# Four pairs of a projection by half products, and a planner that prices two engines by intervals

## The chip, the cores and the metric

The kernel runs on one core of a Trainium2 chip. The metric is the device time of one execution in microseconds. Three runs of the kernel before gave 671.8, 672.92 and 673.86 us; their median, 672.92 us, stands for it. Smaller is better. All data are float32. A matrix product is made as three products of high and low parts (`hi*hi`, `hi*lo`, `lo*hi`) in the format that TensorE reads at full pace, so every weight and every activation is first split in two by ScalarE (a copy that rounds) and VectorE (a subtraction).

## The reference

One decoder layer: 512 tokens of width 1024, a pooling mixer and an attention with 8 heads of 64, each merged by its own gate, then a feed-forward part of width 2816. What the change touches is `y_nsa`, the attention's output times `w_nsa_out` (512 rows, 1024 columns):

```python
y_nsa = nsa_mixer(...) @ w_nsa_out[l]                       # (512, 512) @ (512, 1024)
x = x + (gate_pool * y_pool + gate_nsa * y_nsa) @ w_out[l]
h = rms_norm(x, ffn_norm_g[l])
gate_pre, val = jnp.split(h @ w_up[l], 2, axis=-1)
x = x + (jax.nn.silu(causal_dwconv(gate_pre, conv_w[l], conv_b[l])) * val) @ w_down[l]
```

## The kernel before

The stages follow each other: input projection; attention, head by head, with the feature stream beside it (key and value features, pooling, gates and `y_pool`); `y_nsa`; the product with `w_out`; 22 blocks of `up`, among them parts of `down`; the rest of `down`. Activations lie transposed, features on 128 partitions and 512 tokens along a row, so an output feature block is 128x512 in one PSUM bank.

**Who sets the order.** The kernel is not written in the order in which it runs. Every operation is noted by a class `Plan` (line 120 on) with its engine, its tiles and a price, and at the end `emit` (391) runs a list schedule over all of them several times, keeps the order that ends first over a few assumed speeds of transfers, and issues each engine's instructions in it. All instructions therefore carry one line in the profile, L434. `price` (206) returns three numbers: how long the operation occupies its engine (`cost`), how much later its result is there (`tail`), and the bytes of a transfer. In `run` the engine is free again at start plus `cost` (343); a consumer on another engine may start at start plus `cost` plus `tail` plus 0.06 us, and one on the same engine at start plus `cost` (266). `dues` (376) then gives each operation of VectorE, ScalarE and the queues a time by which TensorE needs it, and the next round picks by those times. TensorE has two streams in fixed order of their own: `m` (attention and all behind it) and `f` (the feature stream); the planner only chooses which of the two goes next, keeping their progress about equal. A bank of PSUM or a page of SBUF is given out again when its last reader has run; the weights pass through three rings of three buffers (`wraw`, `whi`, `wlo`).

**Attention.** For each head `scores` (1058) makes scores on TensorE, their minimum on VectorE, exponentials on ScalarE, and normalizes on VectorE; `transposes` turns the blocks on TensorE and splits them into `pt` and `pz`; `av` (1098) multiplies with the values into the single bank `av`, its last product being `av<-ptc`; `av_out` (1125) empties that bank: ScalarE copies one half to `ot`, VectorE adds it to the other, giving `oraw`. Products of the feature stream stand between these steps. The gates are `th`; the products `mm<-xh,whi` and `mm<-yph,whi` belong to that stream.

**`y_nsa`.** Its 1024 output features are four pairs `c` of two blocks of 128. A pair that is in `FASTM` (line 58: 0 and 1) is done by half products, a scheme that makes seven products of half height where the plain way makes eight: the pair's weights are cut into four pieces and, by sums of pieces on VectorE (`s3`, `wraw`), recombined into seven; the attention's output is recombined likewise, once (`half_sums`, 1113, giving `osh` and `osl`). Each half product is two steps of three matmuls of 128x256 (`product`, 1177), so a pair has 42. Between them ScalarE and VectorE copy and add halves (`u`, `mm<-tr`). The last two products of a pair (`end1`, `end2`) are held and issued among the next pair's products. Pairs 2 and 3 go the plain way: two blocks of four steps of three matmuls of 128x512, 24 in all. Either way a block is then gated (`tn`, read back from DRAM with `gp`) and split into `mh` and `ml`, the operand of the product with `w_out`.

**`w_out` and on.** For features 0 and 4 the product starts over the first six columns of `mh`, `ml`, before the last two are there (line 1319); then all eight features are finished, residual added (`x`), and split for `up`. Block 0 of `up` is plain, the others go by half products.

Of the kernel before, what the change touches and what calls it, by code (L numbers as in the profile page):

```python
# [19 lines left out]
KD = 8  # L20
# [34 lines left out]
RINGS = {"wraw": 3, "whi": 3, "wlo": 3}  # L55
PLAIN = (0,)
DIRECT = (0,)
FASTM = (0, 1)
AT = (6, 11, 16)
FILL = {f: (0, 0, 0, 0) for f in range(22)}  # L60
FILL.update({f: (0, 1, 1, 0) for f in (7, 9, 10)})
# [30 lines left out]
def _cols(x):  # L92
    n = 1
    for _, c in list(x.ap)[1:]:
        n *= c
    return n
# [23 lines left out]
class Plan:  # L120
# [3 lines left out]
    def __init__(self, nc):  # L124
        self.real = {"PE": nc.tensor, "ACT": nc.scalar, "DVE": nc.vector, "POOL": nc.gpsimd, "SP": nc.sync}
        self.engines = [Engine(self, n) for n in ("PE", "ACT", "DVE", "POOL", "SP")]
        self.ops, self.tag, self.writes, self.reads, self.users = [], {}, {}, {}, {}
        self.caps, self.rank, self.count, self.psum, self.early = {}, {}, {}, set(), {}
        self.fine = set()
        self.stream, self.open, self.after = "m", None, []  # L130
        self.span, self.lead, self.base = [0, 0], LEAD, BASE

# [73 lines left out]
    def price(self, eng, method, outs, ins, a, kw):  # L206
        n = max(_cols(x) for x in outs + ins)
        if method == "dma_start":
            x = outs[0]
            size = x.ap[0][1] * _cols(x) * 4 if hasattr(x, "ap") else 0  # L210
            return (0.87 if eng == "POOL" else 0.45), 0.0, size * (2.0 if kw.get("accum_op") is not None else 1.0)
        if eng == "PE":
            n = _cols(a[2])
            return max(n / 2250.0 + (0.005 if n < 300 else 0.0), 0.109), 0.17, 0
        if eng == "ACT":
            c = 0.19 + n * 0.000835
            if any(_cols(x) == 1 for x in ins):
                c += 0.09
            if kw.get("accum_out") is not None:
                c += 0.19  # L220
            if a[2] in (AF.Sin,):
                c += 1.28
            return c, 0.0, 0
        if eng == "DVE":
            wide = [x for x in ins if _cols(x) > 1]
            if method == "tensor_tensor_reduce":
                return 0.24 + n * 0.00105, 0.0, 0
            if len(wide) > 1 or method == "tensor_reduce" or any(x.tensor.name in self.psum for x in wide):
                return 0.15 + n * (0.00105 if method != "scalar_tensor_tensor" else 0.00114), 0.0, 0
            return 0.2 + n * 0.00054, 0.0, 0  # L230
        if method == "memset":
            return 0.1 + n * 0.0008, 0.0, 0
        return 0.33 + n * 0.0025, 0.0, 0
# [204 lines left out]
def hybrid_layer(ctx: ExitStack, tc: tile.TileContext, xT, xa, pos, par, cst, poolw, w1, wa, wb, wf,  # L438
                 wpo, wno, wout, wup, wdn, wdh, wdz, out):
    nc = tc.nc  # L440
    pl = Plan(nc)
# [49 lines left out]
    def mm3(pt, wh, wl, xh, xl, k0, k1, koff=0, nk=None, first=0):  # L491
        nk = k1 if nk is None else nk
        for k in range(k0, k1):
            c = slice((k - koff) * P, (k - koff + 1) * P)
            with pl.unit():
                PE.matmul(pt, wh[:, c], xh[k], start=(k == first), stop=False)
                PE.matmul(pt, wh[:, c], xl[k], start=False, stop=False)
                PE.matmul(pt, wl[:, c], xh[k], start=False, stop=(k == nk - 1))
# [208 lines left out]
    for t in range(NT):  # L707
        pt = bank("mm")
        tk = slice(t * P, (t + 1) * P)
        for k in range(KD):  # L710
            wh, wl = bw[k]
# [200 lines left out]
    for i in range(2):  # L912
# [8 lines left out]
        for q in range(4):  # L921
            hi, lo = page("w1h", dt=F32R), page("w1l", dt=F32R)
            split(hi, lo, w1t[q])
            for l in range(2 * q, 2 * q + 2):
                c = slice((l % 2) * 256, (l % 2 + 1) * 256)
# [83 lines left out]
    def cmp_scores(g):  # L1009
        cps[g] = page("cs", (P, 4, P))  # L1010
        tmp = page("ct", (P, 4, P))
        for j in range(2):
            pt = bank("tr")
            pq = pt.rearrange("p (q a t) -> p q a t", q=2, a=2)
            with pl.unit():
                for i in range(2):
                    for a in range(2):
                        PE.matmul(pq[:, :, a], kz[:, g, i], QT[a, 2 * j + i][:, 2 * g:2 * g + 2], start=(i + a == 0),
                                  stop=(i == 1), skip_group_check=True)
            r, o = slice(j * 64, (j + 1) * 64), slice((1 - j) * 64, (2 - j) * 64)  # L1020
            t, c = (x.rearrange("p a b -> p (a b)") for x in (tmp, cps[g]))
            ACT.activation(t[r], pt[o], AF.Copy)
            DVE.tensor_add(c[r], pt[r], t[r])
# [34 lines left out]
    def scores(h, i):  # L1058
        g, hh = divmod(h, 4)
        n = i + 1  # L1060
        pt = bank("sc", (P, 4, 2, P)) if n > 2 else bank("tr", (P, 2, 2, P))
        with pl.unit():
            for j in range(0, n, 2):
                m = min(2, n - j)
                for s in range(2):
                    PE.matmul(pt[:, j:j + m], QT[h % 2, i][:, h // 2], KT[s, j // 2, g][:, 0:m], start=(s == 0), stop=(s == 1),
                              skip_group_check=True)
        x = pl.tile(sb, (P, 8, 2, 64), F32, "pp", "ppb", 4) if n > 2 else pl.tile(sb, (P, 4, 2, 64), F32, "pp", "ppa", 2)
        sm = keep("asm", (P, 4, 2), bufs=4)
        pp = [x[:, :2 * n, b].rearrange("p (j u) k -> p j u k", u=2) for b in range(2)]  # L1070
        pt = pt[:, 0:n].rearrange("p j b (u k) -> p j b u k", u=2)
        rows = mask[:, NT - n:NT].rearrange("p j (u k) -> p j u k", u=2)
        for b in range(2):
            DVE.tensor_tensor_reduce(out=pp[b], in0=pt[:, :, b], in1=rows, scale=1.0,
                                     scalar=3.0e38, op0=ALU.add, op1=ALU.min, accum_out=sm[:, 0, b:b + 1])
        for b in range(2):
            ACT.activation(pp[b], pp[b], AF.Exp, bias=sm[:, 0, b:b + 1], scale=-1.0,
                           accum_out=sm[:, 1, b:b + 1])
        DVE.reciprocal(sm[:, 2], sm[:, 1])
        DVE.tensor_mul(sm[:, 3], sm[:, 2], gates[:, i, 3 * h + 1:3 * h + 3])  # L1080
        for b in range(2):
            DVE.tensor_scalar_mul(pp[b], pp[b], sm[:, 3, b:b + 1])
        Pt[h, i] = x
# [54 lines left out]

    compress_kt()
    scores(0, 0)  # L1140
    cmp_scores(0)
    cmp_scores(1)
    scores(0, 1)
# [43 lines left out]
    mh, ml, nots, held = [None] * KD, [None] * KD, [], []  # L1187
# [9 lines left out]
    for c in range(4):  # L1197
        if c not in FASTM:
            more = list(held)
            del held[:]  # L1200
            wh, wl = weights(flat(wno[c]), 1024, "v")
# [80 lines left out]

        held.extend((end1, end2))
        tail = nots[-1]
    for q in held:
        q()

    x2, gh, gl, begun = [None] * KD, [None] * KD, [None] * KD, []
    acc = page("acc")
# [29 lines left out]
    for f in (0, 4):  # L1319
        wh, wl = weights(flat(wout[f]), 1024, "v")  # L1320
        begin[f] = wh, wl, any_bank()
        mm3(begin[f][2], wh, wl, mh, ml, 0, 6, nk=KD)
    for f in (0, 4, 1, 5, 2, 6, 3, 7):
        xres = page("xres")
        with pl.behind(tail):
# [254 lines left out]
        held.extend((end1, end2))  # L1580

    for f in range(KF):
        if f in AT:
            g = AT.index(f)
            (hp_group if g == HALVED else dn_group)(g)
        fill(FILL[f][0], True)
        if f in PLAIN:
            up_plain(f)
        else:
            up_fast(f, *FILL[f][1:])  # L1590
# [140 lines left out]
```

## Time and profile before

| what | before |
|---|---|
| median of three runs, us | 672.92 (671.8 to 673.86) |
| the profiled execution, us | 672.4 |
| its span from first to last instruction, us | 670.6 |
| granted TensorE clock | 1.000 |
| TensorE busy, us (share) | 665.8 (99%) |
| VectorE busy, us | 568.5 (85%) |
| ScalarE busy, us | 470.5 (70%) |
| GpSimd busy, us | 111.8 (17%) |
| VectorE busy from head 0's `oraw` to head 4's (139.25 to 215.94) | 63.34 of 76.69 |
| VectorE busy from the last `oraw` to the first `x` (262.31 to 297.77) | 30.14 of 35.46 |

In a row of the timeline stand the start in us from the span's start, the duration, the engine (PE is TensorE, PEld its weight loads, DVE VectorE, ACT ScalarE, POOL GpSimd, SP the engine whose queue most transfers use), the operation, the written tile and those read, the shapes, how many, and in brackets how long the engine had been idle and what ended that. Names of tiles on TensorE carry the PSUM tag of the bank (`mm`, `tr`, `av`, `sc`). Instructions of one engine may overlap, so a duration is not the distance to the next start. TensorE's products are pipelined: their durations overlap, their starts give the pitch.

### The profile page before, as it was taken

How to read it: one execution, taken by the hardware profiler on the slowest of the kernel's cores; microseconds unless marked ns; L12 is line 12 of the kernel's file. 1: busy time of each engine (PE TensorE's matmuls, PEld its weight loads, DVE VectorE, ACT ScalarE, POOL GpSimd, SP SyncE). 2: the span in 40 equal slices, each digit the busy share in tenths (PEclk: the TensorE clock that was granted, in tenths of full speed). 3: DMA queues.
4: the chain of work that ended last, by engine and by line, in shares of the span. 5: the costliest groups of instructions: out<-in, count | busy, mean ns of one | idle time of the engine just before them, and what ended most of it. 6: DMA issues, size and time to landing. Idle time of an engine off the chain costs nothing.

```text
span 670.6 us, 12179 instructions
## 1 busy us (share of the span) xinstructions
PE 665.8 (99%) x4338; PEld 606.0 (90%) x4338; DVE 568.5 (85%) x1271; ACT 470.5 (70%) x887; POOL 111.8 (17%) x138
## 2 busy tenths in 40 slices
PE   9999999999999999999999999999999999999997
PEld 8898888888888888988899999999999999998997
DVE  6879988888888787888888998988898998889883
ACT  7676967776677775447788777767867877776751
POOL 0010211111110010001332222122312323221120
PEclk9999999999999999999999999999999999999999
DMA  8468965645545553956976868777867897885574
GB/s 309 148 167 233 255 174 154 181 107 146 124 138 132 142 127 108 328 165 204 250 170 145 206 150 219 171 197 162 199 159 173 182 217 175 174 188 151 143 175 109
DMA packets 52140, 118.26 MB, mean 176 GB/s; under 512 B 6000, under 2 KB 10224, under 8 KB 52080
## 3 DMA queue, kind: packets, MB, share of 16 engines
q1 hardware_dynamic: 33072, 77.23, 35.7%
q0 software_dynamic: 18864, 40.12, 33.2%
q8 instruction: 34, 0.56, 0.3%
q14 instruction: 26, 0.21, 0.1%
q10 hardware_dynamic: 144, 0.14, 0.1%
HBM read 70.28 MB, written 6.29 MB: 114 GB/s over the span
## 4 chain that ended last, share of the span: by engine, by line
PE 99%; DMA 1%; ACT 0%; DVE 0%; issue 0%
PE mm L434 40%; PE tr L434 36%; PE sc L434 12%; PE av L434 11%; DMA x<-xa 1%; ACT xh L434 0%; DVE o L434 0%
## 5 line engine op out<-in xcount | busy, mean ns | idle before, releaser
L434 ACT ACTIVATE whi<-wraw 128x1024 fp32r<-128x1024 f32 (+4 forms) x99 | 91.6, 928 | 32.3 <-PE sc L434 14.3
L434 DVE TENSOR_TENSOR wlo<-wraw,whi 128x1024 fp32r<-128x1024 f32 (+3 forms) x73 | 73.7, 1014 | 4.2 <-ACT whi L434 3.8
L434 PE MATMUL tr<-tl,sh 128*128 128x256 f32 x261 | 73.5, 282 | 0.0
L434 PE MATMUL tr<-th,sl 128*128 128x256 f32 x250 | 70.5, 282 | 0.0
L434 PE MATMUL tr<-th,sh 128*128 128x256 f32 x250 | 70.5, 282 | 0.0
L434 PE MATMUL mm<-xh,whi 128*128 128x512 f32 x176 | 70.4, 400 | 0.0
L434 PE MATMUL mm<-xh,wlo 128*128 128x512 f32 x176 | 68.8, 391 | 0.0
L434 PE MATMUL mm<-xl,whi 128*128 128x512 f32 x176 | 68.7, 390 | 0.0
L434 POOL DMA_DIRECT2D sl<-r x46 | 39.6, 862 | 142.7 <-ACT sl L434 106.0
L434 POOL DMA_DIRECT2D wlo<-wraw x26 | 22.4, 860 | 223.7 <-ACT wlo L434 179.6
L434 PEld LDWEIGHTS tr<-tl,sh 128*128 128x128 f32 x261 | 49.1, 188 | 0.2
L434 PEld LDWEIGHTS tr<-th,sh 128*128 128x128 f32 x250 | 47.0, 188 | 0.5
L434 PEld LDWEIGHTS tr<-th,sl 128*128 128x128 f32 x250 | 47.0, 188 | 0.0
L434 ACT ACTIVATE wlo<-wraw 128x1024 fp32r<-128x1024 f32 x26 | 27.6, 1060 | 19.7 <-PE mm L434 18.4
L434 POOL DMA_DIRECT2D sl<-wraw x30 | 25.9, 863 | 86.6 <-ACT sl L434 62.2
L434 PEld LDWEIGHTS mm<-xh,wlo 128*128 128x128 f32 x176 | 33.1, 188 | 7.3
L434 PEld LDWEIGHTS mm<-xl,whi 128*128 128x128 f32 x176 | 33.1, 188 | 6.0
L434 PEld LDWEIGHTS mm<-xh,whi 128*128 128x128 f32 x176 | 33.1, 188 | 6.1
L434 ACT ACTIVATE sh<-wraw 128x512 fp32r<-128x512 f32 x56 | 34.8, 621 | 4.2 <-DVE wraw L434 4.0
L434 ACT ACTIVATE pp<-pp,asm 128x256 f32<-128x256 f32 (+3 forms) x64 | 35.2, 554 | 2.1 <-DVE asm L434 2.0
L434 DVE SCALAR_TENSOR_TENSOR ft<-fg,pr,ft 128x511 f32<-128x511 f32 (+1 forms) x44 | 32.8, 746 | 2.9 <-ACT ft L434 2.5
L434 ACT ACTIVATE sh<-r 128x512 fp32r<-128x512 f32 x50 | 31.0, 620 | 1.5 <-ACT sh L434 0.9
(468 smaller groups left out, 2193.6 us busy)
## 6 DMA issues: line engine op xcount, KB each, us to landing
wlo<-wraw POOLq DMA_DIRECT2D x26, 512.0 KB, 4.8
wraw<-wup SPq DMA_DIRECT2D x23, 512.0 KB, 4.3
sl<-r POOLq DMA_DIRECT2D x46, 256.0 KB, 5.4
wraw<-wf SPq DMA_DIRECT2D x22, 512.0 KB, 3.9
r<-wup SPq DMA_DIRECT2D x42, 256.0 KB, 5.5
sl<-wraw POOLq DMA_DIRECT2D x30, 256.0 KB, 4.3
wraw<-wdn SPq DMA_DIRECT2D x16, 320.0 KB, 3.7
sl<-s POOLq DMA_DIRECT2D x17, 256.0 KB, 5.0
```

Of the source, the lines that this page charges most:

```text
L434: getattr(self.real[o.eng], method)(*a, **kw)
```

## The change

Three things are done.

1. `FASTM` is 0 to 3: pairs 2 and 3 of `y_nsa` go by half products too. Per pair 24 matmuls of 128x512 become 42 of 128x256, and the sums, splits and half evictions that pairs 0 and 1 have are added.
2. The two held products of the last pair, which were issued right behind it, now stand inside the start of `w_out`: behind the first four columns of feature 0, which need only pairs 0 and 1.
3. The planner's price gets a switch, `tight`. While it is on, ScalarE's cost is 0.09 us lower (0.19 with an accumulator) and its tail 0.1, and VectorE's cost is 0.08 lower with a tail of 0.08. It is turned on behind the first scores of attention, so for every operation noted from there, and off where block 1 of `up` begins. The feature stream is noted earlier and keeps the old prices.

```diff
-FASTM = (0, 1)
+FASTM = (0, 1, 2, 3)
...
-        self.fine = set()
+        self.fine, self.tight = set(), 0
...
         if eng == "ACT":
-            c = 0.19 + n * 0.000835
+            c = 0.19 - 0.09 * self.tight + n * 0.000835
...
             if kw.get("accum_out") is not None:
-                c += 0.19
+                c += 0.19 - 0.1 * self.tight
...
-            return c, 0.0, 0
+            return c, 0.1 * self.tight, 0
         if eng == "DVE":
+            less = 0.08 * self.tight
             wide = [x for x in ins if _cols(x) > 1]
             if method == "tensor_tensor_reduce":
-                return 0.24 + n * 0.00105, 0.0, 0
+                return 0.24 - less + n * 0.00105, less, 0
             if len(wide) > 1 or method == "tensor_reduce" or any(x.tensor.name in self.psum for x in wide):
-                return 0.15 + n * (0.00105 if method != "scalar_tensor_tensor" else 0.00114), 0.0, 0
-            return 0.2 + n * 0.00054, 0.0, 0
+                return 0.15 - less + n * (0.00105 if method != "scalar_tensor_tensor" else 0.00114), less, 0
+            return 0.2 - less + n * 0.00054, less, 0
...
     scores(0, 0)
+    pl.tight = 1
     cmp_scores(0)
...
-    for q in held:
-        q()
...
         begin[f] = wh, wl, any_bank()
-        mm3(begin[f][2], wh, wl, mh, ml, 0, 6, nk=KD)
+        mm3(begin[f][2], wh, wl, mh, ml, 0, 4, nk=KD)
+        while held:
+            held.pop(0)()
+        mm3(begin[f][2], wh, wl, mh, ml, 4, 6, nk=KD)
...
     for f in range(KF):
+        if f == 1:
+            pl.tight = 0
```

The new prices move instructions on every engine. Two places matter.

**TensorE, where head 0 ends.** `sc<-kt,qt` are scores of a later head, `tr<-cs,pp` the transposes of the next head, `mm<-xh` products of the feature stream, `av<-pt` the next head's first product into the bank `av`. Before, behind head 0's last product:

```order
L434 MATMUL av<-ptc,cst 128x512
L434 MATMUL sc<-kt,qt 128x512 x4
L434 MATMUL mm<-xh,whi 128x512
L434 MATMUL mm<-xl,whi 128x512
L434 MATMUL mm<-xh,wlo 128x512
```

Those last three rows stand four times there, then the transposes, two scores, and the three rows four times again, before `av<-pt`. In the change:

```order
L435 MATMUL av<-ptc,cst 128x512
L435 MATMUL sc<-kt,qt 128x512 x4
L435 MATMUL tr<-cs,pp 128x128 x8
L435 MATMUL mm<-xh,whi 128x512
L435 MATMUL mm<-xl,whi 128x512
L435 MATMUL mm<-xh,wlo 128x512
L435 MATMUL mm<-pmh,pwh 128x512
L435 MATMUL mm<-pml,pwh 128x512
L435 MATMUL mm<-pmh,pwl 128x512
L435 MATMUL sc<-kt,qt 128x512 x2
L435 MATMUL sc<-kt,qt 128x256 x2
L435 MATMUL av<-pt,vv 128x512
```

Six wide products instead of 24 stand between `av<-ptc` and the next `av<-pt`. From head 0's `av<-ptc` to head 4's there are 72 fewer of them than before; behind the last head's, 60 stand ahead of `y_nsa`, where 27 stood.

**VectorE, ahead of the first gating of `y_nsa`.** `wraw`, `s`, `sh`, `sl` and `wlo` are sums and low parts of a pair's weights, `th` the gates of the feature stream, `tn` the gating of pair 0. Before:

```order
L434 TENSOR_TENSOR osl<-tb,osh 128x512
L434 TENSOR_TENSOR wlo<-wraw,whi 128x512
L434 TENSOR_TENSOR wraw<-wraw 128x256 x2
L434 SCALAR_TENSOR_TENSOR th<-th,mm 128x512
L434 TENSOR_TENSOR wlo<-wraw,whi 128x512
L434 TENSOR_TENSOR wlo<-wraw,whi 128x1024
L434 TENSOR_TENSOR u_728<-tr,u_728 128x256
L434 SCALAR_TENSOR_TENSOR tn<-tn,tr 128x256
```

In the change, the last rows ahead of that gating:

```order
L435 SCALAR_TENSOR_TENSOR th<-th,mm 128x512
L435 TENSOR_TENSOR wlo<-wraw,whi 128x512
L435 TENSOR_TENSOR s_770<-wraw 128x256
L435 TENSOR_TENSOR wraw<-wraw 128x256
L435 TENSOR_TENSOR sh<-s_770,sh 128x256
L435 SCALAR_TENSOR_TENSOR th<-th,mm 128x512
L435 TENSOR_TENSOR wlo<-wraw,whi 128x512
L435 TENSOR_TENSOR wraw<-wraw 128x256 x2
L435 TENSOR_TENSOR sl<-wraw,sh 128x512
L435 SCALAR_TENSOR_TENSOR tn<-tn,tr 128x256
```

Much of the weights of pairs 2 and 3 is prepared ahead of the first gating. From the last `oraw` to the first `x` VectorE has 78 instructions, where it had 50.

## The prediction

> **What bounds the kernel now.** I read the page first (busy time and the chain of what ended last), then TensorE's own waits.
>
> ```profile
> span 670.6 us, 12179 instructions
> PE 665.8 (99%) x4338; PEld 606.0 (90%) x4338; DVE 568.5 (85%) x1271; ACT 470.5 (70%) x887; POOL 111.8 (17%) x138
> ...
> PE 99%; DMA 1%; ACT 0%; DVE 0%; issue 0%
> ...
> PE mm L434 <- POOL ones L434: 1.0, 1, 1.0
> ```
>
> The last row is TensorE's whole list of waits: once, 1.0 us, before the first product. A busy share alone would prove little, because ends of matmuls are modelled; the missing waits say more, though one shorter than such a modelled end stays hidden (pair 0 below has some). The time is the number of products times their pitch, and every other engine matters only if it makes TensorE wait. So the change can win just what it takes off TensorE, and it can lose without limit. TensorE's timeline in the output projection gives the pitch.
>
> ```profile
> 266.85 0.28 PE L434 MATMUL tr<-oh,whi 128*128 128x256 f32 x1
> ...
> 268.38 0.39 PE L434 MATMUL mm<-osh,whi 128*128 128x256 f32 x1
> ...
> 270.73 0.28 PE L434 MATMUL tr<-oh,whi 128*128 128x256 f32 x1
> ...
> 275.73 0.39 PE L434 MATMUL tr<-oh,whi 128*128 128x512 f32 x1
> ...
> 282.60 0.40 PE L434 MATMUL mm<-oh,whi 128*128 128x512 f32 x1
> ...
> 288.05 0.39 PE L434 MATMUL av<-mh,whi 128*128 128x512 f32 x1
> ...
> 267.96 0.37 ACT L434 ACTIVATE mm<-tr 128x256 f32<-128x256 f32 x1
> ```
>
> The first product of pair 0 starts at 266.85, of pair 1 at 270.73, of pair 2 at 275.73, of pair 3 at 282.60, and of `wout` at 288.05.
>
> **The products.** Between 270.73 and 275.73 stand 42 products of 256 columns: five of pair 1's half products and the two that pair 0 had held back, six matmuls each. That is 5.00 us, 0.119 us a product. Between 282.60 and 288.05 stand the 24 wide products of pair 3 as it is now: 5.45 us, 0.227 us each. Pairs 2 and 3 each replace 24 by 42, so the term is 2 x (5.00 - 5.45) = **-0.9 us**. Its bounds: pair 0 took 3.88 us for 30 products (266.85 to 270.73) where 30 x 0.119 is 3.57, because its half products wait for copies by ScalarE (267.96 to 268.33, ahead of the product at 268.38) with no held product to cover them; if both new pairs lost 0.31 like that, -0.3 remains. I take -0.9: the new pairs stand behind held products, as pair 1 does.
>
> Nothing is loaded more or less: each pair reads one slab of `wno` and the same four 512-wide tiles. ScalarE gets per pair three evictions and more, smaller splits, some 2 us; it is busy for 15.3 of 35.5 us in this stretch (below), which covers them. Without that cover they would cost 4 us.
>
> **The prices.** The second part tells the planner that an instruction frees its engine about 0.08 us (VectorE) or 0.09 us (ScalarE) before its result is there. VectorE's and ScalarE's timelines:
>
> ```profile
> 263.03 0.43 DVE L434 SCALAR_TENSOR_TENSOR ta<-ta,oraw 128x256 f32<-128x256 f32 x1
> 263.50 0.42 DVE L434 SCALAR_TENSOR_TENSOR tb<-ta,oraw 128x256 f32<-128x256 f32 x1
> 263.84 0.42 DVE L434 TENSOR_TENSOR tb<-oraw 128x256 f32<-128x256 f32 x1
> ...
> 265.54 0.69 DVE L434 TENSOR_TENSOR ol<-oraw,oh 128x512 fp32r<-128x512 f32 x1
> 266.14 0.68 DVE L434 TENSOR_TENSOR osl<-tb,osh 128x512 fp32r<-128x512 f32 x1
> 266.74 0.68 DVE L434 TENSOR_TENSOR wlo<-wraw,whi 128x512 fp32r<-128x512 f32 x1
> ...
> 276.03 1.22 DVE L434 TENSOR_TENSOR wlo<-wraw,whi 128x1024 fp32r<-128x1024 f32 x1
> 277.17 0.42 DVE L434 TENSOR_TENSOR u<-av,u 128x256 f32<-128x256 f32 x1
> 277.50 0.41 DVE L434 SCALAR_TENSOR_TENSOR tn<-tn,tr 128x256 f32<-128x256 f32 x1
> ...
> 257.42 0.62 ACT L434 ACTIVATE whi<-wraw 128x512 fp32r<-128x512 f32 x1
> 257.94 0.62 ACT L434 ACTIVATE sh<-wraw 128x512 fp32r<-128x512 f32 x1
> ```
>
> The intervals are real: 265.54 to 266.14 is 0.60 for an instruction of 0.69; 276.03 to 277.17 is 1.14 for 1.22; 277.17 to 277.50 is 0.33 for 0.42; on ScalarE 0.52 for 0.62. But `tb` at 263.50 reads what the instruction ahead of it wrote, and starts 0.47 after it, not 0.34. The planner's rule for a consumer on the same engine (start plus cost, line 266) now promises 0.34. So the old prices were safe everywhere, and the new ones are right for independent neighbours and 0.13 us short for each dependent one. The old plan's safety is what TensorE's empty list of waits shows; the new plan gives it up.
>
> The price alone adds no instruction. What it changes is the order: fewer products of the feature stream between the heads, and 60 of them behind the last head where 27 stand now (the two pieces of the order above are from these places). The work of TensorE is the same. What moves is its cover. Two stretches decide.
>
> **Stretch one: heads 0 to 4 of attention.** I take TensorE from `av<-ptc` of head 0 to that of head 4, and VectorE between the `oraw` of the same heads.
>
> ```profile
> 134.59 0.42 PE L434 MATMUL av<-ptc,cst 128*128 128x512 f32 x1
> ...
> 155.37 0.68 DVE L434 TENSOR_TENSOR oraw<-av,ot 64x512 f32<-64x512 f32 x1
> ...
> 158.14 0.40 PE L434 MATMUL av<-pt,vv 128*128 128x512 f32 x1
> ...
> 213.32 0.42 PE L434 MATMUL av<-ptc,cst 128*128 128x512 f32 x1
> ...
> core 0: us, PE busy (x) PEld busy (x) DVE busy (x) ACT busy (x) POOL busy (x), PEclk, DMA share, GB/s
> 60.95:89.78 28.83, 28.83 (x152) 24.43 (x150) 27.93 (x65) 25.88 (x44) 4.41 (x6) 1.00 0.85 226
> 139.25:215.94 76.69, 76.69 (x414) 64.79 (x413) 63.34 (x198) 55.27 (x121) 6.88 (x8) 1.00 0.53 133
> 262.31:297.77 35.46, 35.46 (x196) 30.95 (x195) 30.14 (x51) 15.29 (x25) 0.00 (x0) 1.00 0.69 233
> ```
>
> TensorE takes 213.32 - 134.59 = 78.7 us. In the new order 72 wide products fewer stand there: 72 x 0.227 = 16.3, so 62.4 us remain. VectorE is busy for 63.3 us (139.25 to 215.94). In the new order it has three 512-wide instructions fewer (-1.8), three 256-wide fewer (-1.0) and two more minima over scores, priced like the nearest row, a 512-wide read of PSUM (+1.2): 61.7 us. It would be needed for **99%** of the time, where it now works 63.3 of 76.7, 83%. The reserve is the lag that it may have: there is one `av` bank, head h+1 writes it, and `oraw` must have read it first. The tightest now is 155.37 + 0.68 = 156.05 against 158.14: 2.1 us. So TensorE waits when VectorE works at less than 61.7 / (62.4 + 2.1) = 96% of this stretch. From 60.95 to 89.78 it worked 27.9 of 28.8 us, 97%, while TensorE waited for nothing: a late VectorE has its inputs ready and stops for nobody. I take 0, between 0 at 97% and, at the 83% of now, 74.3 - 64.5 = 9.8 us.
>
> **Stretch two: from the last head to `wout`.** From the last `oraw` at 262.31 to the first evicted `x` at 297.77 VectorE is busy for 30.1 of 35.5 us.
>
> ```profile
> 271.34 0.42 DVE L434 TENSOR_TENSOR u<-tr,u 128x256 f32<-128x256 f32 x1 [0.47 <-ACT u L434]
> ...
> 272.38 0.42 DVE L434 SCALAR_TENSOR_TENSOR tn<-tn,mm 128x256 f32<-128x256 f32 x1 [0.28 <-PE mm L434]
> ...
> 274.51 0.42 DVE L434 TENSOR_TENSOR u<-tr,u 128x256 f32<-128x256 f32 x1 [0.65 <-PE tr L434]
> ...
> 279.36 0.42 DVE L434 SCALAR_TENSOR_TENSOR tn<-tn,mm 128x256 f32<-128x256 f32 x1 [0.44 <-PE mm L434]
> ...
> 282.09 0.69 DVE L434 SCALAR_TENSOR_TENSOR tn<-tn,tr 128x512 f32<-128x512 f32 x1 [0.41 <-PE tr L434]
> ...
> 297.77 0.69 DVE L434 SCALAR_TENSOR_TENSOR x<-av,xres 128x512 f32<-128x512 f32 x1 [2.41 <-PE av L434]
> ```
>
> The new order has, between the same two points, 24 more instructions of 256 columns (sums of weights, half splits, half evictions: 24 x 0.33 = 7.9), six more of 512 (3.6) and two fewer of 1024 (-2.3): 30.1 + 9.2 = 39.3 us. TensorE offers 35.5 + 33 x 0.227 (the later products, 7.5) - 0.9 = 42.1 us. So 2.8 us of idleness are left, where now there are 5.3: 2.41 at the end, and five short waits of 2.25 together in the middle, which four half-product pairs will have too. What is late next is `ml` of features 6 and 7. The held half products of pair 3 now stand inside the first `wout` block, and 24 wide products (5.4 us) lie between them and the first use of their result, where 36 (8.2 us) lie now; behind that use wait six products, the first `x`, and with it the eviction that frees a bank. The needed `ml` must be done some 1.1 us before `x` (six products less one). VectorE reaches it after 39.3 - 0.6 + 2.25 = 41.0 us, and 42.1 - 1.1 = 41.0 are there. For a tie I take **+0.4 us**, one more wait of the size of those five (0.45 on average); the bounds are 0 and, with twice the middle waits, 43.2 - 41.0 = 2.2.
>
> **The sum.** -0.9 + 0 + 0.4 = -0.5 us against the profiled execution: its 672.4 us become 671.9. That execution lies 0.5 below the median of the runs, 672.92, so I forecast **672.4 us**.
>
> **Rivals.** (1) *VectorE becomes the bound in stretch one.* For it: 99% needed, and the dependent neighbours that the new price leaves out (0.13 us each). Against it: the 97% row. At 90%, halfway between 83 and 97, it needs 61.7 / 0.90 = 68.6 us, 4.1 over the 64.5 that it has; 672.92 - 0.9 + 0.4 + 4.1 = 676.5. It decides from 96% downwards. (2) *The late `ml`.* The middle waits of stretch two double: 2.2 us instead of 0.4, 674.2. For it: twice as many half-product pairs; against it: VectorE that is late waits less. (3) *More than the products is won.* Were no wait added and pair 0's 0.31 us won as well, 671.7; below the 670.9 that would tell it from no change only the spread of the runs (671.8 to 673.86 now) could carry it. (4) *The intervals do not exist*, and an instruction holds its engine to its end. Then each of some 160 instructions in stretch one costs 0.08 us more than above, 13 us, and VectorE needs 74.7 us against 64.5: about 682. The 0.60 us between 265.54 and 266.14 for an instruction of 0.69 speaks against it. [...]
>
> **Chances.** Forecast 0.56, (1) 0.24, (2) 0.14, (3) 0.05, (4) 0.01. What can be told from no change begins at 0.3%, 2.0 us: faster is below 670.9, slower above 674.9. Faster: (3) and the lower spread of the forecast, 0.08. Slower: most of (1), some of (2), (4): 0.25. The same: 0.67. The range reaches from 671.0 (all of -0.9, with 1 us of spread) to 676.0, just short of rival (1).
>
> **What would show it.** Right: TensorE's list of waits stays at the one of 1.0 us; pairs 2 and 3 take 5.0 us each from first product to first product; VectorE's busy share in stretch one is 97% or more, and `oraw` comes later behind `av<-ptc` than now without moving the next `av`. For (1): waits of TensorE in `av` or `sc` behind VectorE, and a stretch of over 64 us from the `av<-ptc` of head 0 to that of head 4. For (2): a wait of `wout`'s products for `ml`. I would be wrong altogether if TensorE waited behind pair 1 of `up`, where prices and code are as they were.

## The result: 677.45 us, slower by 0.6%, and the profile after

The changed kernel took 677.45 us (median of 6 runs, 676.05 to 678.68), the kernel before 672.87 beside it: a ratio of 1.0062, 95% interval 1.0049 to 1.0074. The forecast was 672.4 in a range that ended at 676.0. The profiled execution took 676.82 us. These are the page's rows for span, busy time and the chain that ended last.

```profile
span 674.9 us, 12271 instructions
...
PE 667.5 (99%) x4374; PEld 608.6 (90%) x4374; DVE 576.0 (85%) x1293; ACT 475.8 (70%) x899; POOL 111.2 (16%) x138
...
PE 91%; DMA 4%; DVE 3%; ACT 1%; issue 1%; POOL 0%; SPq 0%; POOLq 0%; ACTq 0%; DVEq 0%
```

TensorE is still busy for 99% of the span, and VectorE's share has not moved. But the chain, which was 99% TensorE, now runs through transfers for 4% (1% before). TensorE's own list of waits says where it is released late (us in total, how often, the longest).

```profile
PE mm L435 <- ACT u L435: 1.8, 1, 1.8
PE sc L435 <- DMA sl<-wraw: 1.1, 1, 1.1
PE mm L435 <- POOL ones L435: 1.0, 1, 1.0
```

The wait of 1.0 us at the start was there before (it stands ahead of eight products of unsplit float32, which took 3.78 us, 0.47 for 128 columns; the first three of high and low parts, right behind them, took 0.42 for 512); the other two are new. To see the whole loss, I added up the distances between the starts of neighbouring products on TensorE, and set against them what the same products take without interruption (0.227 us at 512 columns, 0.118 at 256, about in proportion for the rest; what is taken for the shortest moves single rows by some tenths of a us, in both kernels alike). What lies above is the **excess**, by stretch of the span:

| us | before | after | difference |
|---|---|---|---|
| the products' own time | 645.25 | 644.30 | -0.95 |
| excess up to 116 us | 7.33 | 7.53 | +0.20 |
| excess in attention, 116 to 264 | 11.78 | 11.67 | -0.11 |
| excess in the projection, 264 to 300 | 0.38 | 0.79 | +0.41 |
| excess from 300 us on (`up`, `down`) | 0.85 | 6.05 | **+5.20** |
| ahead of the first product and behind the last one's start | 5.02 | 4.58 | -0.44 |
| span | 670.61 | 674.92 | +4.31 |

Everything that was lost was lost behind 300 us, where the changed kernel makes the same products from the same code at the same prices. TensorE's timeline shows both places.

```profile
471.21 0.28 PE L435 MATMUL sc<-ytl,sh 128*128 128x256 f32 x1
472.54 0.39 PE L435 MATMUL sc<-yth,sl 128*128 128x256 f32 x1 [1.06 <-DMA sl<-wraw]
...
579.77 0.28 PE L435 MATMUL av<-gp,wlo 128*128 128x256 f32 x1
581.81 0.39 PE L435 MATMUL mm<-th,sh 128*128 128x256 f32 x1 [1.75 <-ACT u L435]
...
583.57 0.41 PE L435 MATMUL mm<-oraw,sl 128*128 128x256 f32 x1
583.78 0.41 PE L435 MATMUL mm<-th,sh 128*128 128x256 f32 x1
```

From 471.21 to 472.54 a product took 1.33 us instead of 0.118; from 579.77 to 581.81 another took 2.04. And behind the second one the pitch is 0.21 us (583.57 to 583.78) where it is 0.118 elsewhere. The busy time of each engine in three stretches of 5 us (the number after POOL's column is the granted clock) shows the reason.

```profile
575.00:580.00 5.00, 5.00 (x43) 4.84 (x41) 0.95 (x3) 1.37 (x4) 0.11 (x1) 1.00 0.87 193
580.00:585.00 5.00, 3.25 (x19) 3.19 (x19) 4.91 (x11) 4.62 (x10) 1.15 (x2) 0.78 0.54 120
585.00:590.00 5.00, 5.00 (x40) 5.00 (x39) 3.68 (x7) 3.95 (x8) 2.29 (x3) 0.88 0.80 159
```

The clock in the rows behind the wait is 0.78 and 0.88: from 582.75 to 586.16 TensorE was granted half of it, and that cost 1.6 us more. In the first row VectorE worked 0.95 us of 5 and ScalarE 1.37: both stood still *before* TensorE did. ScalarE's timeline says for what.

```profile
578.68 0.63 ACT L435 ACTIVATE yh<-y 128x512 fp32r<-128x512 f32 x1 [3.63 <-DMA sl<-r]
579.22 0.80 ACT L435 ACTIVATE ft<-fg,pr 128x512 f32<-128x512 f32 x1
579.92 1.04 ACT L435 ACTIVATE whi<-wraw 128x1024 fp32r<-128x1024 f32 x1
580.87 0.61 ACT L435 ACTIVATE sl<-r 128x512 fp32r<-128x512 f32 x1
581.39 0.36 ACT L435 ACTIVATE u<-mm 128x256 f32<-128x256 f32 x1
```

`yh` waited 3.63 us for the transfer `sl<-r`; behind it in ScalarE's order stand three more, and then the eviction `u<-mm`, for which TensorE waits. `yh` reads nothing of `sl` or `r`. That it waits for the page that `r` gives back when the transfer has read it is inferred from how the planner hands out pages; the trace gives only the releaser. The transfer is one of GpSimd's accumulating ones, which finish the low parts of the half products' weights. The issues between 568.3 and 571.3 us (KB each, us from issue to landing):

```profile
sl<-r POOLq DMA_DIRECT2D x2, 256.0 KB, 6.9
wraw<-wup SPq DMA_DIRECT2D x1, 512.0 KB, 4.5
sl<-s POOLq DMA_DIRECT2D x1, 256.0 KB, 7.5
r<-wup SPq DMA_DIRECT2D x1, 256.0 KB, 6.6
```

Five transfers in 2.4 us; the last `sl<-r`, issued at 570.59, landed at 578.58, 8.0 us later, where the median of the 43 between 330 and 640 us is 5.1.

So the theory to test: the new order of `up` leaves transfers less time to land than they need, engines that work in order stand behind them, and TensorE behind those. Its rival: the loss belongs to what the change does, to its products or its prices.

### The profile page after: what moved, and what is told of

It is laid out like the page before. It is cut to its first block, busy times and chain, and to the rows that moved or that the text cites. A ratio compares the mean times of both kernels' runs of the same rounds, so it can differ in the third digit from the quotient of the medians.

```text
span 674.9 us, 12271 instructions
## 1 busy us (share of the span) xinstructions
PE 667.5 (99%) x4374; PEld 608.6 (90%) x4374; DVE 576.0 (85%) x1293; ACT 475.8 (70%) x899; POOL 111.2 (16%) x138
## 4 chain that ended last, share of the span: by engine, by line
PE 91%; DMA 4%; DVE 3%; ACT 1%; issue 1%; POOL 0%; SPq 0%; POOLq 0%; ACTq 0%; DVEq 0%
PE mm L435 40%; PE tr L435 29%; PE sc L435 11%; PE av L435 11%; DMA sl<-r 1%; DMA sl<-wraw 1%; DMA r<-wup 1%; DVE wlo L435 1%; DMA x<-xa 1%; DVE wraw L435 0%; ACT whi L435 0%; POOL sl L435 0%; DVE nrv L435 0%; ACT sh L435 0%; DVE th L435 0%
## 5 line engine op out<-in xcount | busy, mean ns | idle before, releaser
L435 PE MATMUL mm<-tl,sh 128*128 128x256 f32 x231 | 65.7, 284 | 0.0
L435 PE MATMUL mm<-th,sh 128*128 128x256 f32 x210 | 59.8, 285 | 1.8 <-ACT u L435 1.8
L435 PE MATMUL mm<-th,sl 128*128 128x256 f32 x210 | 59.7, 284 | 0.0
L435 PEld LDWEIGHTS mm<-tl,sh 128*128 128x128 f32 x231 | 44.0, 191 | 0.2
L435 PEld LDWEIGHTS mm<-th,sh 128*128 128x128 f32 x210 | 40.0, 191 | 2.4 <-ACT u L435 2.0
L435 PEld LDWEIGHTS mm<-th,sl 128*128 128x128 f32 x210 | 40.1, 191 | 0.0
```

The source lines that it names most:

```text
L435: getattr(self.real[o.eng], method)(*a, **kw)
```

## The experiments

All times stand beside runs of the kernel before on the same chip. The excess is that of each profiled execution.

### Whose order loses

The `up` part of one kernel's order was written into the other as a table, per engine; the part ahead of it was left as the planner drew it.

```diff
+LATER = {
+    "PE": [...],
...
+}
...
-        for o in best[1]:
+        lines = {e: [o for o in best[1] if o.eng == e] for e in LATER}
+        first = self.marks[2]
+        for e, line in lines.items():
+            late = iter(LATER[e])
+            lines[e] = [o if o.i < first else self.ops[first + next(late)] for o in line]
+        order, _ = self.run(start, 0, 0.8, RATE, lines)
+        for o in order:
```

The changed kernel with the `up` order of before:

> The change as it is, but each engine goes through the operations of the `up` and `down` stages (those noted from the first block of `up` on) in the order that the kernel before has; everything ahead of them stays in the change's order. Nothing is left out. Theory A (the loss is two waits of TensorE in the middle of `up`, 1.2 us at 471 and 1.9 us at 580 with a slower granted clock behind the second, and they come from the new order there, not from the three edits): both waits go, the clock is 1.000 again, and the saving of the products is what is left: 671.9 us, ratio 0.9986. Rival B (the extra half products or the 60 late feature products start something that lasts into `up`, in the clock or in the transfers): it stays above 675 us. Rival C (half of it is in attention and the projection, where the list of waits does not see it): 673.5 to 675.

The kernel before with the `up` order of the change:

> The reverse: the kernel before, none of the three edits, but the operations of `up` and `down` go in the order that the change's plan has. Nothing is left out. Theory A: the loss comes along, waits near 471 and 580 and a clock under 1 behind the second, 676 to 678.5 us. Rival B: no loss without the extra products, 672.5 to 673.5. Rival C: about 674.5.

Measured: 673.39 us against 672.47 (1.0009, 1.0000 to 1.0017) for the first, 681.36 (1.013, 1.0117 to 1.0144) for the second. Most of the loss goes where the order goes: with before's order the excess behind 300 us is 2.65 instead of 6.05, and the kernel *without* the change, with the change's order, has 8.82. But neither run came out as theory A said. The first kernel did not reach 671.9, and lies just under rival C's range: 1.8 us of the 2.65 are new compared with before, from the same order. Its waits:

```profile
PE mm L448 <- POOL ones L448: 1.0, 1, 1.0
PE sc L448 <- DMA sl<-wraw: 0.5, 1, 0.5
PE mm L448 <- ACT u L448: 0.5, 2, 0.3
```

The second lies above all three ranges. Its clock stayed at 1.000 and it has no wait at 471. At 582.5 it loses 2.2 us in the way of the change: ScalarE's `yh` had stood still for 2.8 us for `sl<-r`, and the eviction for which TensorE waits is behind it. But another 2.3 us are lost between 336 and 347, where one kernel's order meets the other's. So part of its loss is that of an order put behind a beginning for which it was not drawn, and how much is not shown.

### One half of the change at a time

All four pairs by half products at the old prices (the line `pl.tight = 1` taken out):

> Pairs 2 and 3 by half products and the held ones in their new place, but the planner keeps its old prices throughout. Nothing is left out. Theory A: up to the first block of `up` TensorE has no wait of over 0.5 us and the end of that stretch comes within 1.5 us of the change's; what `up` does is a third draw of its order, so the total is 671.5 plus its waits there, which the trace names, somewhere from 671.5 to 678. Rival D (with the old prices the planner cannot place the sums of two more pairs, and VectorE is late in the projection): waits of 1 to 4 us between the last head and the first `x`.

The new prices with `FASTM = (0, 1)` and the held products back behind their pair:

> The new prices alone: pairs 2 and 3 go the plain way. Nothing is left out. Theory A: attention shows no wait of over 0.5 us although VectorE has little time to spare there, the stretch up to `up` takes as long as in the kernel before within 1 us; the total is 672.9 plus the waits that this fourth draw has in `up`, 672.5 to 679. Rival E (prices without the 0.13 us of dependent neighbours starve TensorE in attention): 2 us or more of waits between 100 and 260.

Measured: 676.2 us (1.0053, 1.0037 to 1.0068) and 675.35 (1.0039, 1.0024 to 1.0055). Either half alone is slower than before. Without the prices the excess in the projection is 3.37 us (0.79 in the change): TensorE waits for `ml` and `u` of VectorE.

```profile
PE tr L435 <- DVE ml L435: 0.9, 2, 0.5
PE av L435 <- DVE u L435: 0.9, 1, 0.9
```

So rival D is right, and in these two orders the prices save 2.6 us of what the products would cost there. With the prices alone, theory A is right on attention and rival E falls: the excess there is 11.51 us, before 11.78. And both runs have a new excess behind 300 us, 3.21 and 2.75, though neither touches that part: each drew it anew.

### One eviction earlier

In the changed kernel `u<-mm` is moved from behind `sl` to directly behind `yh`.

```diff
-        for o in best[1]:
+        lines = {e: [o for o in best[1] if o.eng == e] for e in ("PE", "ACT", "DVE", "POOL", "SP")}
+        line = lines["ACT"]
+        line.remove(self.ops[3416])
+        line.insert(733, self.ops[3416])
+        order, _ = self.run(start, 0, 0.8, RATE, lines)
+        for o in order:
```

> The changed kernel with one ScalarE instruction in another place: the eviction `u<-mm` that TensorE waited for at 579.8 us stood behind `yh`, `ft`, `whi` and `sl`; it now stands directly behind `yh`. Everything else on every engine is in the changed kernel's order. Theory F (ScalarE works in order, and what is queued ahead of the eviction holds TensorE): `yh` began at 578.68 us and takes about 0.5, so `u` is done by 579.6, before TensorE asks for the bank at 579.8; the wait of 1.9 us goes, and with it the 1.65 us of slower clock behind it, if the clock falls because TensorE stood still: 677.45 - 3.5 = about 673.9 us. Rival G (the clock falls there by itself): only the wait goes, about 675.5. Rival H (the late transfer holds so much else up, VectorE's queue of 4 us above all, that TensorE waits for something else a few products later): 676.5 to 677.5.

Measured: 676.55 us (1.0058, 1.0045 to 1.0071). Rival H is right. `u` ran at 577.45 and TensorE did not wait for it; but 12 products later it waits 2.0 us for the next eviction, `mm<-av`, which stands behind the same queue. ScalarE's timeline:

```profile
576.91 0.63 ACT L440 ACTIVATE yh<-y 128x512 fp32r<-128x512 f32 x1 [3.61 <-DMA sl<-r]
577.45 0.37 ACT L440 ACTIVATE u<-mm 128x256 f32<-128x256 f32 x1
...
580.89 0.63 ACT L440 ACTIVATE ft<-ft 128x512 f32<-128x512 f32 x1 [0.39 <-DVE ft L440]
581.42 0.37 ACT L440 ACTIVATE mm<-av 128x256 f32<-128x256 f32 x1
```

What stands behind 3.6 us of standing still is late as a whole here, and moving one instruction did not help.

### Other draws

The kernel before with another draw, two of the planner's six starting delays changed; then the changed kernel and the kernel before with a rehearsal at later landings.

```diff
-LANDS = (0.8, 0.8, 1.2, 1.2, 2.0, 2.0)
+LANDS = (0.8, 0.8, 1.2, 1.2, 1.6, 1.6)
```

> The kernel before, with nothing changed but two of the six landing delays that the planner's draws start from (2.0, 2.0 become 1.6, 1.6): same products, same prices, another order drawn. Theory D (the loss is that a re-drawn order of `up` is chosen in rehearsals with landings of at most 1.4 us and is too tight for the chip's): rehearsed with 2.0 us this order loses 4.5 us of TensorE in `up`, the order before 1.3, the changed kernel's 11.1 (measured 0.1 and 5.0), so it should lose about 2 us in `up`: 674.5 us, 673.5 to 676. Rival E (the loss belongs to the change itself, its products or its prices): 672.5 us, no difference from before.

```diff
-MORE = 4
+MORE = 12
...
-LANDS = (0.8, 0.8, 1.2, 1.2, 2.0, 2.0)
-TRIALS = ((0.5, RATE), (0.8, RATE), (1.4, RATE), (0.8, 0.9 * RATE))
+LANDS = (0.5, 0.8, 1.0, 1.4, 1.8, 2.2)
+TRIALS = ((0.5, RATE), (0.8, RATE), (1.4, RATE), (0.8, 0.9 * RATE), (2.0, RATE))
```

> The changed kernel, with the planner alone altered: a fifth rehearsal with landings of 2.0 us, start delays of 0.5 to 2.2 us, and 12 more draws a stage in place of 4. Products, prices and the place of the held work are the changed kernel's. Theory D (the loss is the draw): the order now chosen loses 1.2 us in `up` when rehearsed at 2.0 us, as the order before does (1.3; measured 0.1); then the 0.95 us of shorter products stay won and stretch two costs its 0.3: 672.0 us, 671.3 to 673, at or below the kernel before. Rival E (the loss belongs to the products or prices): 676 to 678, as the changed kernel.

> The kernel before with the planner altered exactly as for the changed kernel with the later rehearsal: fifth rehearsal with landings of 2.0 us, start delays of 0.5 to 2.2 us, 12 more draws in place of 4. Products, prices and the held work are those of before. Theory D (a newly drawn order costs what it costs, whoever draws): rehearsed at 2.0 us it loses 2.2 us in `up`, the changed kernel's order by this rule 1.2 (measured 674.87 us), so 674 to 677, about 675.3: no faster than the changed kernel by the same rule. Rival E (the change's products or prices make it slower): it stays at 672.5, some 2.4 us faster than the changed kernel by the same rule.

Measured, with what the planner's own rehearsal makes of each order (TensorE's idle time in `up` if every transfer lands so many us after its bytes):

| order | rehearsed at 0.8 | at 1.4 | at 2.0 | excess behind 300 us | time, us | ratio to before |
|---|---|---|---|---|---|---|
| before | 0.73 | 0.73 | 1.31 | 0.85 | 672.6 | |
| change | 0.14 | 1.83 | 11.08 | 6.05 | 677.45 | 1.0062 |
| before, another draw | 0.18 | 0.18 | 4.46 | 4.61 | 676.12 | 1.0050 (1.0038 to 1.0062) |
| change, later rehearsal | 0.50 | 0.50 | 1.19 | 6.79 | 674.87 | 1.0038 (1.0023 to 1.0052) |
| before, later rehearsal | 0.22 | 0.22 | 2.15 | 1.79 | 673.35 | 1.0011 (1.0003 to 1.0020) |

The second draw of the kernel before is the plainest run of all: no product, no price, no held work differs, and it is 3.5 us slower, 0.1 above the range of theory D. Rival E said 672.5. At landings of 0.8 us, the middle of those by which the planner chose, that order and the change's looked *better* than before's (0.18 and 0.14 against 0.73). The waits of that second draw come about as the change's do. At 579.8 us TensorE waits for an eviction, and three instructions ahead of it in ScalarE's order `yh` had stood still for `sl<-r`:

```profile
PE tr L434 <- ACT u L434: 1.5, 2, 0.9
...
577.19 0.63 ACT L434 ACTIVATE yh<-y 128x512 fp32r<-128x512 f32 x1 [2.76 <-DMA sl<-r]
```

The later rehearsal is a miss in both directions. It took some 2 us off the changed kernel, not the 5.4 expected; its runs scatter from 673.75 to 678.0, and the profiled one is the slowest, with waits at 492.7 and 593.9 us, the first of them behind VectorE, which had stood still for 3.0 us for `sl<-r`. And it cost the kernel before 0.75 us, not 2.7. So a uniform delay of 2.0 us tells the change's order from before's, but not a good draw from a middling one. By this one rule the changed kernel is some 1.8 us slower than the kernel before, where theory D said that it would be no slower and rival E that it would be 2.4 us slower. This pair of runs speaks for rival E, though it is one draw of each; that the change makes bad draws likelier is neither shown nor excluded.

### The transfers themselves

The order of each kernel was written out as a table for all engines, and the accumulating transfers of the half products in `up` were halved.

```diff
-    def split_by_dma(hi, lo, x):
+    def split_by_dma(hi, lo, x, rows=P):
         ACT.activation(lo, x, AF.Copy, scale=-1.0)
-        POOL.dma_start(lo, x, accum_op=ALU.add)
+        POOL.dma_start(lo[:rows], x[:rows], accum_op=ALU.add)
...
-                split_by_dma(hi, lo, x)
+                split_by_dma(hi, lo, x, 64)
```

> The changed kernel with its own order on every engine, written out as a table; the accumulating transfers that finish the low parts `sl` of the half products in `up` carry 64 of the 128 partitions. So half of each low part is left uncorrected, the output is off by that, and nothing else is left out: every instruction, wait and place in the queues is kept, only the bytes of these transfers are halved. Theory T (TensorE's loss in `up` comes from these transfers landing late): the excess over the products' own time in `up`, 5.7 us in the changed kernel and 0.9 in the kernel before, falls to about 1; 677.45 - 4.7 = 672.7 us, 672.0 to 673.5. Rival U (the new order is too tight for ScalarE or VectorE, whatever the transfers do): 676 to 678.

> The control for the halved transfers: the kernel before with its own order, and the same 64 of 128 partitions in the same transfers (half of each low part left uncorrected). It hardly waits in `up` as it is (0.9 us over the products' own time, 0.5 of it present in every kernel), so both theories expect no difference: 672.5 us, 672.0 to 673.0. A gain of over 1 us would mean that less traffic helps TensorE in some other way, and would take its share out of the run beside it.

Measured: 671.93 us for the change (0.9985, 0.9976 to 0.9993), 672.97 for the control (1.0001, 0.9992 to 1.0010). Theory T is right, and a little short: with the instructions of the change in the change's order on every engine, and only fewer bytes in 89 transfers, over 5 us are gone. It is not the writing out of the order that did it: the kernel with one eviction moved was issued from the change's fixed order in the same way, with all bytes, and stayed at 676.55. The issues between 330 and 640 us, of the change and then of this run:

```profile
sl<-r POOLq DMA_DIRECT2D x43, 256.0 KB, 5.1
r<-wup SPq DMA_DIRECT2D x38, 256.0 KB, 5.3
...
sl<-s POOLq DMA_DIRECT2D x15, 256.0 KB, 5.0
```

```profile
r<-wup SPq DMA_DIRECT2D x38, 256.0 KB, 4.4
...
sl<-r POOLq DMA_DIRECT2D x43, 128.0 KB, 3.9
...
sl<-s POOLq DMA_DIRECT2D x15, 128.0 KB, 4.1
```

These halved ones land 1.2 and 0.9 us sooner, the untouched loads `r` beside them 0.9. TensorE's list of waits is down to the one at the start:

```profile
PE mm L448 <- POOL ones L448: 1.0, 1, 1.0
```

The control shows that fewer bytes are worth nothing where nobody waits. With these transfers halved the change is worth 0.85 us against the kernel before.

### One load later

The same order lost 1.8 us more in the changed kernel than in before. In both, GpSimd's transfer `sl<-wraw` goes out at 465, and the load `wraw<-wdh` follows as soon as a buffer of its ring is free. The timeline of the kernel before, and its issue of that transfer (us to landing last):

```profile
465.15 0.86 POOL L434 DMA_DIRECT2D sl<-wraw  x1 [2.35 <-DVE sh L434]
467.18 0.33 SPq L434 DMA_DIRECT2D wraw<-wdh  x1
```

```profile
sl<-wraw POOLq DMA_DIRECT2D x1, 256.0 KB, 4.5
```

The same two views of the changed kernel with the order of before:

```profile
464.93 0.85 POOL L448 DMA_DIRECT2D sl<-wraw  x1 [2.36 <-DVE wraw L448]
465.35 0.33 SPq L448 DMA_DIRECT2D wraw<-wdh  x1
```

```profile
wraw<-wdh SPq DMA_DIRECT2D x1, 512.0 KB, 6.3
sl<-wraw POOLq DMA_DIRECT2D x1, 256.0 KB, 6.9
```

In the second kernel the load left 0.4 us behind the transfer, not 2.0, and the transfer took 6.9 us, not 4.5. It left earlier because the accumulating transfer ahead of it, which frees the buffer, had landed *sooner*, at 465.22 instead of 467.04. The changed kernel has the same at its first wait (465.09 and 465.40, 7.4 us). In the experiment ScalarE issues that load. The forecast below says behind its two `whi<-wraw`; in the order it stands between them (466.61, the load at 466.81, 467.15):

```diff
-                SP.dma_start(rg, flat(wdh[c]))
+                (ACT if c == 1 else SP).dma_start(rg, flat(wdh[c]))
...
-    "ACT": [..., 2818, 2713, ...],
+    "ACT": [..., 2818, 2869, 2713, ...],
```

> The changed kernel with the order of before in `up` (673.39 us against 672.47), every instruction in the same place but one: the load `wraw<-wdh` that SyncE issued at 465.35 us, 0.4 us after the accumulating transfer `sl<-wraw` (464.93), is issued by ScalarE behind its two `whi<-wraw`, so at about 467.0, as in the kernel before (467.18, where the transfer landed in 4.5 us, not 6.9). Theory K (the two transfers slow each other, and the wait of 0.7 us at 471 is theirs): the transfer lands by 470.5, that wait goes, 672.7 us. Rival L (the transfer is late by itself, or another one takes the place): the wait stays or moves, 673.4.

Measured: 672.34 us (0.9993, 0.9983 to 1.0002), 1.05 us under the kernel that it was made from, and not told from the kernel before. The wait at 471 is gone; the issues of the two transfers:

```profile
wraw<-wdh ACTq DMA_DIRECT2D x1, 512.0 KB, 4.5
sl<-wraw POOLq DMA_DIRECT2D x1, 256.0 KB, 4.0
```

Theory K is right in what it says of the wait. But the load went out at 466.81, only 0.8 us behind the transfer (465.99), and through another engine's queue; whether the distance or the queue made the difference is open.

### Two more evictions

From that kernel's waits at 589.0 and 599.4 us, two evictions `u<-mm` moved ahead in ScalarE's order:

```diff
-    "ACT": [..., 3516, 3491, ..., 3583, 3585, 3586, 3566, ...],
+    "ACT": [..., 3491, 3516, ..., 3566, 3583, 3585, 3586, ...],
```

> The kernel of the later load (672.34 us) with two more ScalarE instructions moved ahead: the evictions `u<-mm` for which TensorE waited 0.3 us at 589.0 and 0.9 us at 599.4 stood behind `sh<-wraw` (held by a late transfer) and behind `sl<-r`, `sh<-r`, `sh<-wraw`; each now runs once its products are done (by about 588.0 and 598.5). Theory F (what is queued ahead of the eviction holds TensorE): both waits go, 672.34 - 1.2 = 671.1 us, about 1.5 us below the kernel before, which is what the shorter products and the shorter tail were worth. Rival H (as with the eviction moved at 580 us, another instruction that stands behind a late transfer takes the place): 672.0 to 672.6.

Measured: 671.98 us against 672.94 (0.9986, 0.9977 to 0.9994): the one kernel of this study that moves all its bytes and is faster than both, 1.0 us faster than the kernel before. Theory F held for the waits. This is its whole list:

```profile
PE mm L444 <- POOL ones L444: 1.0, 1, 1.0
PE tr L444 <- ACT xh L444: 0.4, 1, 0.4
```

The excess behind 300 us fell from 2.29 to 1.33. The time fell by less than the 1.2 expected, some 0.5 us by the two ratios: the profiled execution from which I took the waits, 674.36 us, was the longest of that kernel's 12, so the waits were probably shorter in the others. The two intervals overlap, so that half microsecond is not clear of the spread. That here the waits went with the evictions moved and at 580 us they did not fits the rows: there ScalarE had stood still for 3.6 us, here for 0.7 and not at all.

## Why the prediction was wrong

- **The products, -0.9: right.** The own time fell by 0.95. The first products of pairs 1, 2, 3 and of `wout` start at 270.99, 275.99, 280.99 and 285.99: 5.00 us for each pair.

```profile
270.99 0.28 PE L435 MATMUL tr<-oh,whi 128*128 128x256 f32 x1
...
275.99 0.28 PE L435 MATMUL tr<-oh,whi 128*128 128x256 f32 x1
...
280.99 0.28 PE L435 MATMUL tr<-oh,whi 128*128 128x256 f32 x1
...
285.99 0.39 PE L435 MATMUL tr<-mh,whi 128*128 128x512 f32 x1
```

- **Stretch one, 0: right, and close.** From head 0's `av<-ptc` at 133.43 to head 4's at 195.83 TensorE takes 62.4 us, the number forecast. VectorE is busy for 61.27 of the 64.52 us between the same heads' `oraw`, 95%. I asked for 97% or more, and had TensorE wait below 96%; neither came. VectorE needed 0.4 us less than I had counted and, from 1.1 us behind `av<-ptc` at head 0, it fell back to 3.2 at head 4. That is all of the 2.1 us of lag that I allowed, but at head 4 the next `av<-pt` came later too and left 4.4 us. The tightest reserve of the bank fell from 2.1 to 1.7 us (head 2); none was used up, and rivals (1) and (4) fall. By the estimate under rival (4), 74.7 us of VectorE against 64.5, this stretch would have been about ten us longer; the 62.4 us disagree with that.
- **Stretch two, +0.4: the size right, by luck in part.** The excess rose by 0.41; VectorE is busy for 40.1 of 43.1 us to the first `x` where 39.3 of 42.1 were forecast. But the wait that I priced, for `ml` of features 6 and 7, did not come. Pair 0 loses 0.27 us ahead of `mm<-osh,whi` (0.11 before), one product of `wout` starts 0.11 late behind `ml` of feature 4, and the rest is spread over many products. Rival (2) falls.

```profile
134.53:199.05 64.52, 64.52 (x363) 54.71 (x362) 61.27 (x196) 51.27 (x118) 5.17 (x6) 1.00 0.44 111
254.21:297.32 43.11, 43.00 (x268) 38.68 (x267) 40.13 (x79) 22.05 (x41) 0.00 (x0) 1.00 0.59 204
```

- **The end, not in the sum: -0.44.** What lies behind the last product's start went from 4.03 to 3.59 us; that part was drawn anew too.
- **The step that failed** is the one that the sum does not contain. I priced everything behind pair 1 of `up` at nothing, and wrote that I would be "wrong altogether if TensorE waited behind pair 1 of `up`, where prices and code are as they were". Prices and code are, but the *order* is not: the planner draws the whole program, and another beginning gave another `up`. I had put "the old plan's safety" down to the old prices; it was a property of that one order, down to when its transfers meet. Its price was +5.2 us, more than all terms of the sum, and no rival stood for it. My rivals asked whether engines had enough time; the run with halved transfers shows that in `up` they had, and that the transfers had not. The kernel before, drawn anew without any change, lost 3.5 us in the same way.
- **What stays open:** why the transfer that frees the ring's buffer landed in 3.5 us in one kernel and 5.1 in the other, with the same issues 1.5 us behind it; whether the change makes bad draws likelier; and what the 1.8 us are that before's order loses in the changed kernel, of which the moved load explains the wait at 471 alone. The run with halved transfers changes their bytes and all other traffic's share at once; it shows that late landing is the cause, not which transfer is the first of the chain.

## What to carry to other kernels

Where a planner sets the order, every edit is two edits: what it says, and a new draw of all that comes behind it; separate them by putting one kernel's order under the other's code, and price a new draw as a term of its own unless the old order is kept (here 0.75 and 3.5 us for two new draws of an unchanged kernel). An order that shows no idle time in a rehearsal is not safe when the trace's transfers land later than the rehearsal's; and a rehearsal with all of them late by the same time did not find a good order here either (1.19 us rehearsed, 6.79 measured). And when TensorE waits for an eviction, look at what stands ahead of it on that engine: in the cases here moving the one instruction took the wait away where its engine was busy or had stood still for 0.7 us, and not where it had stood still for 3.6.

## What was unexpected in the hardware

Behind some waits TensorE went at half pace for 3.41 us (pitch 0.21 instead of 0.118; in the change the granted clock was 0.50 from 582.75 to 586.16) and lost 1.6 us more: after waits of 1.91 us (the change), 2.14 (one eviction earlier, clock 0.76 from 580 to 585 and 0.90 from 585 to 590) and 2.06 (later rehearsal, clock 0.66 from 495 to 500), the same amount each time; after 1.80 (later rehearsal) and 2.22 (before with the change's order), with the clock at 1.00 in the stretches of 5 us around and behind them, it lost no more than 0.2. So in three of these five cases a wait of some 2 us cost 3.5 to 3.7. In the clock records of the traces each stretch at full pace or, between two of them, at half pace lasts a whole number of 3.413 us (195 in the kernel before; 169, then one at half pace, then 26 in the change). What sets the two waits that cost nothing more apart from the other three is not shown: the longest of the five is one of them.

Transfers of the same kind and size (256 KB, accumulating) took from 3.2 or 3.3 to 8.0 us to land in either kernel. By an estimate with the planner's own model of the queues, fed with the issue times of the changed kernel's trace, a transfer's bytes are through a median of 1.0 us before it lands, which is within the 0.5 to 1.4 that the planner rehearses, but about one transfer in ten is over some 1.9 us late (172 transfers between 330 and 640 us; before: 0.9 and 1.9). It is that tenth that an order has to survive.
